# Loads ahead of the masks, row sums of squares on VectorE, a shared transfer rate and an earlier place for the output projections in a planned trunk kernel

## The chip, the cores and the metric

The kernel runs on one core of a Trainium2 chip. The metric is the device time of one execution in microseconds (us). The engines are named as in the profile: PE is TensorE (PEld its weight loads), DVE VectorE, ACT ScalarE, POOL GpSimd, and SP the engine that issues all DMAs here.

## The reference

Two layers of a hybrid trunk over 1024 positions of width 1024, in float32. Every layer normalises, projects into two mixers, projects back, adds the residual, and runs a gated MLP (width 2816) whose gate passes a causal convolution:

```python
for l in range(DEPTH):                       # DEPTH = 2
    h = rms_norm(x, norm_mix_pre[l])
    if l % 2 == 0:
        z = h @ ev_w_in[e]
        ya, v_a = rwkv7_mix(...)             # 8 heads x 64, a recurrence over time
        yb = sgu_mix(...)                    # spatial gating on blocks of 128
        mix = jnp.concatenate([ya, yb], axis=-1) @ ev_w_out[e]
    else:
        z = h @ od_w_in[o]
        yc = hgrn2_mix(...)                  # gated linear recurrence
        yd = gdn_mix(...)                    # gated delta rule
        mix = jnp.concatenate([yc, yd], axis=-1) @ od_w_out[o]
    x = x + rms_norm(mix, norm_mix_post[l])
    h = rms_norm(x, norm_ffn_pre[l])
    x = x + rms_norm(conv_glu_ffn(h, ...), norm_ffn_post[l])
```

## The kernel before

**Tiling.** The positions are cut into two halves of 512 (`TH`); activations lie with the features on the 128 partitions, so a tile is 128x512. A product of float32 accuracy is made of three products of a shorter type: `split` writes the high part of a tile (`h`, or `wh` of a weight; on ScalarE) and the rest (`l`, or `wl`; on VectorE), and `dense` multiplies h by wh, l by wh, and h by wl into a PSUM bank `d`. A block of 128 output columns takes 24 such multiplications over a depth of 1024. All other multiplications (transposes, the recurrences' small products, norms) go into banks `m`.

**Threads and a planner.** `Trunk.run` makes one Python generator ("thread") for each piece of work: `start` (input and first norm), `rows` (transposes of the raw input for the residual), `sgu`, `mixers` (input projections of the recurrent mixers, which put a `unit` for each head pair and quarter of the positions in a queue), `mix` (output projection, post-norm, residual and next norm: `mixed` and `residual`), and `ffn`, each for a layer and a half. `Plan` keeps a model of the engines. At each step it takes of the threads that can run earliest the one with the smallest urgency (`self.urg`; units 0, `mix` 1, `mixers` 2, `ffn` 3) and `place` gives each instruction a start in the model's time, with a cost by engine and shape. The instructions of each engine are then ordered by these starts, and the order is fixed by dependences, so every engine works strictly in the planned order, whatever happens on the chip. A DMA's arrival in the model is its issue plus 1.1 us plus its bytes over a rate.

**A unit.** A recurrent unit inverts triangular 64x64 matrices. The 16x16 blocks of the diagonal are inverted on GpSimd by `inverse_base`, which sends the matrix through DRAM (`ib`, then `iN`), runs 15 steps of two instructions (`itm`, `iPT`), and sends the result back through DRAM (`ir`, `iR`). TensorE and VectorE finish it (`iU`, `iQ`, `iP`), and then a chain of state steps follows over four chunks of 64 positions (`Z`, `WT`, `ST`, `QT`).

**The head.** `setup` makes constants; the masks `lm` of the inversion are made by GpSimd and VectorE from scratch tiles (`low`, `bk16` to `bk64`) of a pool that is closed again, so that its room goes to the pool `tp` opened next, from which all working tiles come. `start(0)` loads x in eight tiles `xt` of 128x512, then a row of column constants (`columns(0)`: `colr`, transposed into `col`), then small parameters, and normalises (`junk`, `ss`, `xr`), transposes (`m<-ident,xr`) and splits the result into `h` and `l`.

**The residual.** `square_sum` squares a tile on ScalarE and adds it to the running sum on GpSimd. In `residual` this is done for the eight 128x512 tiles `row` of a half after each `row` is scaled and added to `xt`; the sum is then reduced over the partitions by TensorE (`m<-ones,sq`), and the next norm's `xn`, `h` and `l` follow. The feed-forward's convolution keeps the last two columns of the gate `g` in `fhalo`: two small GpSimd instructions in each block.

In the profile nearly all instructions have the line L66, that of the recording helper, so they are told apart by their tiles.

Of the kernel before, what the change touches and what calls it, by code (L numbers as in the profile page):

```python
# [9 lines left out]
F32 = mybir.dt.float32  # L10
F32R = mybir.dt.float32r
AF = mybir.ActivationFunctionType
ALU = mybir.AluOpType
# [80 lines left out]
    return key[1] if key[0] == "base" else key  # L94


class Plan:


# [2 lines left out]
    def __init__(self, nc, past=None, tc=None):  # L102
        self.nc, self.past, self.tc = nc, past, tc
        names = ("tensor", "vector", "scalar", "gpsimd", "sync")
        for n in names:
            setattr(self, n, Engine(self, n, getattr(nc, n)))
        self.busy = {n: [(0.0, 0.0)] for n in names}
        self.ready, self.used, self.uses, self.owner = {}, {}, {}, {}
        self.port = {"vector": [], "gpsimd": []}
        self.now, self.cur = 0.0, None  # L110
        self.fresh, self.given = {}, {}
        self.shared, self.ended, self.turns, self.work = {}, set(), {}, {}
        self.order = {}

        self.lives, self.bufs, self.seq, self.spawned = {}, {}, 0, {}
        self.free = {g: [0.0] * n for g, n in past.bufs.items()} if past else None
# [131 lines left out]
    def place(self, eng, method, outs, ins, scaled=False, func=None):  # L248
        c = self.cost(eng, method, outs[0], ins, scaled)
        t = 0.0  # L250
# [8 lines left out]
        for x in outs:  # L259
            if x.space == DRAM:  # L260
                continue
            n = x.tensor.name
# [36 lines left out]
        t = at  # L299
# [21 lines left out]
        if eng == "tensor":  # L321
            self.now = max(self.now, t) if t - c <= self.now + 0.5 else self.now + c
        elif eng == "sync":
            eng = "dma"
            c = max(0.1, outs[0].size() * 4 / (359e3 if min(outs[0].shape[-1], ins[0].shape[-1]) > 64 else 180e3))
            t = begin + 1.1 + c
        for x in outs:
            n = x.tensor.name
            if t >= self.ready.get(n, (0.0, eng))[0]:
# [7 lines left out]
    def start(self, x, threads):  # L337


        t = max(x.wake, self.now)  # L340
        if not self.past:
            return t
        p = x.piece + 1
        need = self.past.need.get((x.key, p), {})
        for g, n in need.items():
            f = self.free[g]
            if len(f) < n:
                return None
            t = max(t, f[n - 1])
        tags = [g for g in need if g in "BCS"]  # L350
        if tags and not self.safe(x, threads):
            return None
        return t
# [66 lines left out]
class Trunk:  # L420
# [30 lines left out]
    def setup(self):  # L451
# [46 lines left out]

        self.lm = [cst.tile([P, 64], F32, name=f"lm{j}") for j in range(2)]
        self.ibufs, self.icount = {}, {}  # L500
        with ExitStack() as c:
            tmp = self.pool("msk", 1, ctx=c)
            low = tmp.tile([64, 64], F32, name="low")
            nc.gpsimd.memset(low, 1.0)
            nc.gpsimd.affine_select(out=low, in_=low, compare_op=ALU.is_gt, fill=0.0, base=0,
                                    pattern=[[-1, 64]], channel_multiplier=1)
            blks = []
            for w in (16, 32, 64):
                b = tmp.tile([64, 64], F32, name=f"bk{w}")
                nc.gpsimd.memset(b, 1.0)  # L510
                v = b.rearrange("p (n w) -> p n w", w=w)
                nc.gpsimd.affine_select(out=v, in_=v, compare_op=ALU.is_ge, fill=0.0, base=0,
                                        pattern=[[-w, 64 // w], [0, w]], channel_multiplier=1)
                nc.gpsimd.affine_select(out=v, in_=v, compare_op=ALU.is_ge, fill=0.0, base=w - 1,
                                        pattern=[[w, 64 // w], [0, w]], channel_multiplier=-1)
                blks.append(b)
            for j in range(2):
                t = self.lm[j]
                nc.vector.tensor_tensor(out=t[0:64], in0=blks[j + 1], in1=blks[j], op=ALU.subtract)
                nc.vector.tensor_tensor(out=t[0:64], in0=t[0:64], in1=low, op=ALU.mult)  # L520
                nc.vector.tensor_tensor(out=t[0:64], in0=self.ident[0:64, 0:64], in1=t[0:64], op=ALU.subtract)
                nc.vector.tensor_copy(t[64:128], t[0:64])


        self.rst = cst.tile([P, NCH, C], F32, name="rst")
# [7 lines left out]
        self.halo = cst.tile([P, 12, 3], F32, name="halo")  # L533
        self.fhalo = cst.tile([P, MFF, 2], F32, name="fhalo")
        self.tp = self.pool("tp")

    def columns(self, part):

# [174 lines left out]
    def square_sum(self, s, x):  # L713

        sq = self.t("sq")
        self.nc.scalar.activation(sq, x, AF.Square)
        if s is None:
            return sq
        self.nc.gpsimd.tensor_tensor(out=s, in0=s, in1=sq, op=ALU.add)
        return s  # L720

    def inv_rms(self, s):
# [1109 lines left out]
        return x  # L1832

    def start(self, hf):
        self.xss[hf] = xs = self.first_loads(hf)
        if hf == 0:
            self.columns(0)
            self.rwkv_lora()
        yield from self.first_norm(hf, xs)
        self.ready.add((0, hf))  # L1840
        if hf == 0:
            self.columns(1)

    def rows(self, hf):
# [3 lines left out]
    def run(self):  # L1848
# [5 lines left out]
            for n in "rgh":  # L1854
                self.st[(n, j, 0)] = None
        self.groups, self.workers, self.ahead = [5, 5, 4, 4, 4], 4, 1
        self.urg = dict(unit=0, mix=1, sgu=1, mixers=2, ffn=3, start=1, rows=2.5)
        threads = []

        def add(kind, l, hf, gen, cond):  # L1860
# [69 lines left out]
```

## Time and profile before

| what | us |
|---|---|
| median of 3 runs (lowest to highest) | 2994.29 (2992.13 to 2996.55) |
| the profiled execution's own time | 2990.66 |
| its span, first to last instruction | 2988.9 |
| mean granted TensorE clock, share of full speed | 0.976 |
| PE busy | 2835.0 (95%) |
| DVE busy | 1810.9 (61%) |
| ACT busy | 1256.0 (42%) |
| POOL busy | 699.8 (23%) |

The span is what the trace covers; the execution's own time is 1.76 us longer. Busy times are sums over the instructions of an engine. A busy PE is not a PE at full speed: where the granted clock is low, the same multiplications take longer and count as busy all the same.

### The profile page before, as it was taken

The numbers are of one execution on the slowest core, as the hardware profiler recorded it, in microseconds if no ns is written. First come the engines' busy times: TensorE is split into PE (matmuls) and PEld (weight loads), VectorE is DVE, ScalarE is ACT, GpSimd is POOL, SyncE is SP. The second block draws the span as 40 slices with busy tenths as digits, with TensorE's granted clock in tenths as the row PEclk, the third lists the DMA queues.
The fourth block names the chain that finished last, engine by engine and source line by source line (L and its number), as shares of the span: only waits on it lengthen the run. The fifth ranks groups of instructions, "written<-read, shape, count | busy, mean of one in ns | idle before, by whom it ended". The sixth has DMA issues, their size and how long they took to land. (4 is left out here: it accounts for less than half of the span.)

```text
span 2988.9 us, 46564 instructions
## 1 busy us (share of the span) xinstructions
PE 2835.0 (95%) x16608; PEld 2281.5 (76%) x16608; DVE 1810.9 (61%) x3654; ACT 1256.0 (42%) x2435; POOL 699.8 (23%) x1624
## 2 busy tenths in 40 slices
PE   6998999889999999999999999999999999999998
PEld 5776777567878878777778878787777788888886
DVE  5747665765565466565665575666676548454444
ACT  4435354444444345433333344543333335444333
POOL 1255242533020020223430121213443112100001
PEclk9999999899999999999999999999999999999999
DMA  5233353322443344535423443363642344343332
GB/s 160 79 85 80 74 145 95 91 53 76 125 131 102 96 128 95 94 58 79 79 67 92 129 134 113 101 107 70 79 83 60 91 122 144 108 125 89 110 95 92
DMA packets 560229, 294.14 MB, mean 98 GB/s; under 512 B 103293, under 2 KB 533198, under 8 KB 559998
## 3 DMA queue, kind: packets, MB, share of 16 engines
q1 hardware_dynamic: 559998, 291.17, 38.6%
q8 instruction: 131, 2.15, 0.3%
q14 instruction: 100, 0.82, 0.1%
HBM read 255.37 MB, written 35.71 MB: 97 GB/s over the span
## 5 line engine op out<-in xcount | busy, mean ns | idle before, releaser
L66 PE MATMUL d<-h,wh 128*128 128x512 f32 (+1 forms) x2544 | 1049.5, 413 | 2.5 <-ACT h L66 2.3
L66 PE MATMUL d<-h,wl 128*128 128x512 f32 (+1 forms) x2544 | 1016.5, 400 | 14.6 <-DVE wl L66 14.5
L66 PE MATMUL d<-l,wh 128*128 128x512 f32 (+1 forms) x2544 | 1014.1, 399 | 0.2 <-DVE l L66 0.2
L66 ACT CAST wh<-wr 128x512 fp32r<-128x512 f32 (+1 forms) x860 | 507.1, 594 | 702.3 <-PE d L66 539.4
L66 DVE TENSOR_TENSOR wl<-wr,wh 128x512 fp32r<-128x512 f32 (+1 forms) x860 | 568.8, 675 | 245.3 <-ACT wh L66 236.5
L66 PEld LDWEIGHTS d<-h,wl 128*128 128x128 f32 (+1 forms) x2544 | 484.3, 190 | 130.5 <-DVE wl L66 17.9
L66 PEld LDWEIGHTS d<-h,wh 128*128 128x128 f32 (+1 forms) x2544 | 485.6, 191 | 110.3 <-ACT h L66 3.7
L66 PEld LDWEIGHTS d<-l,wh 128*128 128x128 f32 (+1 forms) x2544 | 486.0, 191 | 100.3 <-DVE l L66 2.8
L66 PE MATMUL d<-mh,wh 128*128 128x512 f32 x704 | 284.5, 404 | 0.0
L66 PE MATMUL d<-mh,wl 128*128 128x512 f32 x704 | 279.4, 397 | 3.1 <-DVE wl L66 3.1
L66 PE MATMUL d<-ml,wh 128*128 128x512 f32 x704 | 279.4, 397 | 0.0
L66 POOL TENSOR_TENSOR sq<-sq 128x512 f32<-128x512 f32 x97 | 133.9, 1381 | 540.0 <-ACT sq L66 539.7
L66 DVE SCALAR_TENSOR_TENSOR t<-g,col,t 128x512 f32<-128x512 f32 x176 | 137.2, 780 | 184.1 <-ACT t L66 152.4
L66 POOL TENSOR_TENSOR rt<-rt,mhalf 128x4 f32<-128x4 f32 (+1 forms) x94 | 105.8, 1127 | 459.5 <-DVE rt L66 435.7
L66 POOL TENSOR_TENSOR itm<-iN,iPT 16x39 f32<-16x39 f32 (+15 forms) x480 | 164.3, 342 | 192.7 <-DMA iN<-ib 123.0
L66 DVE TENSOR_TENSOR acc<-acc,d 128x512 f32<-128x512 f32 x128 | 88.0, 687 | 144.4 <-PE d L66 143.9
L66 POOL TENSOR_TENSOR iPT<-iPT,itm 16x55 f32<-16x55 f32 (+15 forms) x480 | 166.1, 346 | 36.1
L66 PEld LDWEIGHTS d<-mh,wl 128*128 128x128 f32 x704 | 133.4, 190 | 36.1 <-DVE wl L66 4.8
L66 PEld LDWEIGHTS d<-mh,wh 128*128 128x128 f32 x704 | 133.5, 190 | 30.8 <-issue 0.4
L66 PEld LDWEIGHTS d<-ml,wh 128*128 128x128 f32 x704 | 133.6, 190 | 29.3 <-DVE ml L66 0.3
L66 ACT COPY g<-d 128x512 f32<-128x512 f32 x88 | 51.6, 586 | 154.8 <-PE d L66 154.6
L66 POOL COPY fhalo<-g 128x2 f32<-128x2 f32 x44 | 9.6, 218 | 391.5 <-ACT g L66 369.7
(339 smaller groups left out, 3206.4 us busy)
## 6 DMA issues: line engine op xcount, KB each, us to landing
wr<-in_ffn_w_in SPq DMA_DIRECT2D x352, 256.0 KB
wr<-in_od_w_in SPq DMA_DIRECT2D x128, 256.0 KB
wr<-in_ffn_w_out SPq DMA_DIRECT2D x96, 256.0 KB
wr<-in_ev_w_in SPq DMA_DIRECT2D x84, 256.0 KB
xt<-xd SPq DMA_DIRECT2D x56, 256.0 KB
wr<-in_ffn_w_out SPq DMA_DIRECT2D x64, 192.0 KB
wr<-in_ev_w_out SPq DMA_DIRECT2D x32, 256.0 KB
yl<-yd SPq DMA_DIRECT2D x32, 256.0 KB
```

Of the source, the lines that this page charges most:

```text
L66: r = fn(*args, **kw)
```

## The change

Four edits. `masks` becomes a method of its own whose scratch tiles are ordinary tiles of `tp` (class "S", up to 128 columns), and is called in `start(0)` after the first norm; `columns(0)` is called ahead of the x loads. The running sum of squares is added on VectorE. In the plan, transfers no longer run side by side at 359 (or 180) KB per us each: `fit_in` puts each into the first free gap of one common list, at 300 (or 150) KB per us. And the thread `mix` gets the urgency -1, so that it stands ahead of the units.

```diff
+def fit_in(iv, t, c):
+
+    i = len(iv)
+    while i > 0 and iv[i - 1][1] > t:
+        i -= 1
+    while i < len(iv) and iv[i][0] < t + c:
+        t = max(t, iv[i][1])
+        i += 1
+    iv.insert(i, (t, t + c))
+    if len(iv) > 200:
+        del iv[:100]
+    return t
...
         elif eng == "sync":
             eng = "dma"
-            c = max(0.1, outs[0].size() * 4 / (359e3 if min(outs[0].shape[-1], ins[0].shape[-1]) > 64 else 180e3))
-            t = begin + 1.1 + c
+
+            c = max(0.1, outs[0].size() * 4 / (300e3 if min(outs[0].shape[-1], ins[0].shape[-1]) > 64 else 150e3))
+            t = fit_in(self.moved, begin + 1.1, c) + c
...
-        with ExitStack() as c:
-            tmp = self.pool("msk", 1, ctx=c)
-            low = tmp.tile([64, 64], F32, name="low")
...
+    def masks(self):
+
+        nc = self.nc
+
+        def square(name):
+            return self.t(name, (64, 128))[:, 0:64]
+
+        low = square("low")
...
-        self.nc.gpsimd.tensor_tensor(out=s, in0=s, in1=sq, op=ALU.add)
+        self.nc.vector.tensor_tensor(out=s, in0=s, in1=sq, op=ALU.add)
...
     def start(self, hf):
+        if hf == 0:
+            self.columns(0)
         self.xss[hf] = xs = self.first_loads(hf)
         if hf == 0:
-            self.columns(0)
             self.rwkv_lora()
         yield from self.first_norm(hf, xs)
         self.ready.add((0, hf))
         if hf == 0:
+            self.masks()
             self.columns(1)
...
-        self.urg = dict(unit=0, mix=1, sgu=1, mixers=2, ffn=3, start=1, rows=2.5)
+        self.urg = dict(unit=0, mix=-1, sgu=1, mixers=2, ffn=3, start=1, rows=2.5)
```

Since the planner sets every engine's order, the edits show in the orders of the instructions more than in their number.

The first place is the head of the program, SP's queue. Before, it began so:

```order
L66 DMA xt<-in_x 128x512 x8
L66 DMA wup<-in_rwkv_w_up 32x512
L66 DMA colr<-in_norm_mix_pre 8x128
L66 DMA mu_168<-in_rwkv_mu 64x1
L66 DMA wup<-in_rwkv_a_up 32x512
L66 DMA gup<-in_rwkv_g_up 96x512
L66 DMA mu_168<-in_rwkv_mu 96x1
L66 DMA wr<-in_ev_w_in 128x4x128 x2
```

The column load `colr` stood behind the eight x loads and one small load. The new queue of SP at the same place:

```order
L66 DMA xt<-in_x 128x512 x5
L66 DMA colr<-in_norm_mix_pre 8x128
L66 DMA xt<-in_x 128x512 x3
L66 DMA mu_141<-in_rwkv_mu 64x1
L66 DMA wup<-in_rwkv_w_up 32x512
L66 DMA gup<-in_rwkv_g_up 96x512
L66 DMA wr<-in_ev_w_in 128x4x128 x2
```

The column load moved up between the fifth and the sixth x load, and two small loads moved behind the first two weights `wr`.

The second place is VectorE in the first output projection (layer 0, first half), where each block ends with a copy `row<-d`; `iU`, `ST` and `Z` are steps of units, `wl` weight parts. Before, its second part read:

```order
L66 TENSOR_TENSOR wl<-wr,wh 128x512
L66 COPY row<-d 128x512
L66 TENSOR_TENSOR iU<-m,lm_105 128x256
L66 TENSOR_TENSOR iU<-m,lm_106 128x256
L66 TENSOR_TENSOR wl<-wr,wh 128x512
L66 TENSOR_TENSOR iU<-m,lm_106 128x256
L66 TENSOR_TENSOR wl<-wr,wh 128x512
L66 TENSOR_TENSOR ST<-U_5621,m 64x128
L66 COPY row<-d 128x512
L66 SCALAR_TENSOR_TENSOR Z_5637<-m,dg,Zd 64x64 x2
L66 TENSOR_TENSOR wl<-wr,wh 128x512
```

Between two `row` copies stood up to four steps of units. The new order of VectorE there:

```order
L66 COPY row<-d 128x512
L66 TENSOR_TENSOR wl<-wr,wh 128x512
L66 TENSOR_TENSOR sq<-sq 128x512
L66 TENSOR_TENSOR wl<-wr,wh 128x512
L66 COPY row<-d 128x512
L66 TENSOR_TENSOR wl<-wr,wh 128x512
L66 TENSOR_TENSOR sq<-sq 128x512
L66 TENSOR_TENSOR wl<-wr,wh 128x512
L66 COPY row<-d 128x512
```

No step of a unit stands between the copies any more, and the sums of squares `sq<-sq` are new on this engine.

The third place is GpSimd at the first halo copy of the feed-forward (layer 0, first half). Before, it stood inside an inversion:

```order
L66 TENSOR_TENSOR itm<-iN,iPT 32x8x8
L66 TENSOR_TENSOR iPT<-iPT,itm 32x8x8
L66 TENSOR_TENSOR itm<-iN,iPT 32x7x9
L66 MEMSET g 128x2
L66 COPY fhalo<-g 128x2
L66 TENSOR_TENSOR iPT<-iPT,itm 32x7x9
```

The rows `itm` and `iPT` are steps of one unit's inversion. The new order of GpSimd there:

```order
L66 MEMSET iPT 32x256
L66 MEMSET iPT 32x16
L66 TENSOR_TENSOR rt<-rt,mhalf 128x4 x2
L66 MEMSET g 128x2
L66 COPY fhalo<-g 128x2
L66 TENSOR_TENSOR itm<-iN,iPT 32x15
L66 TENSOR_TENSOR iPT<-iPT,itm 32x15
L66 TENSOR_TENSOR itm<-iN,iPT 32x14x2
```

The first halo copy now stands ahead of the first step of the inversion that follows; the next one (not shown) stands behind nearly all of that inversion's steps.

## Rows read from the trace of the kernel before

**Rows 1.** The page, part 1: busy time, share, instructions of each engine.

```profile
PE 2835.0 (95%) x16608; PEld 2281.5 (76%) x16608; DVE 1810.9 (61%) x3654; ACT 1256.0 (42%) x2435; POOL 699.8 (23%) x1624
```

**Rows 2.** Stretches: length, engines' busy us (instructions), granted clock, DMA share, GB/s.

```profile
0.00:29.66 29.66, 6.81 (x34) 5.67 (x34) 14.78 (x52) 11.61 (x25) 7.62 (x31) 1.00 0.60 171
29.66:100.00 70.34, 70.34 (x348) 56.04 (x346) 40.35 (x95) 32.70 (x62) 4.40 (x4) 1.00 0.41 113
100.00:546.00 446.00, 414.12 (x3510) 330.20 (x3508) 301.88 (x799) 204.03 (x463) 182.41 (x434) 0.96 0.37 99
546.00:622.00 76.00, 51.13 (x439) 37.76 (x438) 42.18 (x95) 24.37 (x53) 45.87 (x126) 0.80 0.24 58
622.00:2988.90 2366.90, 2292.61 (x12287) 1851.87 (x12286) 1411.69 (x2617) 983.35 (x1835) 459.52 (x1031) 0.98 0.40 98
```

**Rows 3.** Waits of SP's queue up to 30 us: total, times, longest.

```profile
SPq L66 <- DVE lm L66: 5.2, 1, 5.2
```

**Rows 4.** Timeline of the head: start, us, engine, operation, idle before and releaser.

```profile
0.88 0.07 DVE L66 MEMSET mhalf<- 128x8 f32 x1 [0.88 <-PEq L1919]
...
6.02 3.72 SPq L66 DMA_DIRECT2D xt<-in_x  x8
...
6.82 0.59 DVE L66 MEMSET colr<- 128x128 f32 x4
8.78 1.28 ACT L66 ACT_TABLE_LOAD   x1 [8.78 <-DMA xt<-in_x]
...
16.62 0.45 PE L66 MATMUL m<-ident,colr 128*128 128x128 f32 x1 [16.62 <-DMA colr<-in_norm_mix_pre]
...
17.10 0.29 DVE L66 COPY col<-m 128x128 f32<-128x128 f32 x1 [5.51 <-PE m L66]
```

**Rows 5.** The page, part 5: busy us, mean ns, idle us before, releaser.

```profile
L66 POOL TENSOR_TENSOR sq<-sq 128x512 f32<-128x512 f32 x97 | 133.9, 1381 | 540.0 <-ACT sq L66 539.7
...
L66 DVE TENSOR_TENSOR acc<-acc,d 128x512 f32<-128x512 f32 x128 | 88.0, 687 | 144.4 <-PE d L66 143.9
```

**Rows 6.** Timelines of four engines from 545 to 555 us.

```profile
545.45 0.63 ACT L66 ACTIVATE sq<-row 128x512 f32<-128x512 f32 x1
...
551.23 1.25 POOL L66 TENSOR_TENSOR sq<-sq 128x512 f32<-128x512 f32 x1
...
552.53 1.87 PE L66 MATMUL m<-ones,sq 128*128 128x1 f32 x8 [6.30 <-POOL sq L66]
...
554.44 0.16 DVE L66 TENSOR_SCALAR rt<-m 128x4 f32<-128x4 f32 x1 [4.85 <-PE m L66]
```

**Rows 7.** Timelines of DVE and POOL in a later residual stage.

```profile
856.95 0.69 DVE L66 TENSOR_TENSOR row<-row,xt 128x512 f32<-128x512 f32 x1
...
859.98 1.31 POOL L66 TENSOR_TENSOR sq<-sq 128x512 f32<-128x512 f32 x1 [7.20 <-ACT sq L66]
...
860.01 1.82 DVE L66 TENSOR_TENSOR row<-row,xt 128x512 f32<-128x512 f32 x1
```

**Rows 8.** Sum of five residual stages (853:882, 1098:1125, 1728:1756, 1868:1896, 2475:2500).

```profile
sum 137.00, PE 122.87 PEld 96.62 DVE 119.17 ACT 70.69 POOL 57.59; mean PE 24.57 PEld 19.32 DVE 23.83 ACT 14.14 POOL 11.52
```

**Rows 9.** The chain that ended last: start, us, what.

```profile
2632.53 322.70 PE d L66 x1392
```

**Rows 10.** Timelines of POOL, DVE and PE from 592 to 614 us.

```profile
592.49 0.70 POOL L66 TENSOR_TENSOR itm<-iN,iPT 32x15 f32<-32x15 f32 x1 [19.65 <-DMA iN<-ib]
...
610.94 1.71 DVE L66 SCALAR_TENSOR_TENSOR t<-g,col,t 128x512 f32<-128x512 f32 x2 [13.38 <-POOL g L66]
...
613.12 0.77 PE L66 MATMUL m<-ST,QT 128*128 128x128 f32 x2 [11.31 <-DVE ST L66]
```

**Rows 11.** Three stretches of small multiplications alone, columns as in rows 2.

```profile
578.60:594.10 15.50, 14.16 (x313) 12.01 (x311) 13.18 (x37) 7.72 (x20) 1.37 (x4) 1.00 0.24 57
241.80:266.50 24.70, 17.26 (x116) 13.91 (x115) 21.09 (x68) 13.40 (x37) 14.81 (x41) 0.72 0.31 92
...
sum 60.30, PE 50.32 PEld 41.38 DVE 45.25 ACT 29.11 POOL 17.84; mean PE 16.77 PEld 13.79 DVE 15.08 ACT 9.70 POOL 5.95
```

More of the change, by code (lines that the diff above doesn't have):

```diff
@@ L109, in __init__ @@
         self.port = {"vector": [], "gpsimd": []}
+        self.moved = []
         self.now, self.cur = 0.0, None
@@ L500, in setup @@
         self.ibufs, self.icount = {}, {}
-        with ExitStack() as c:
-            tmp = self.pool("msk", 1, ctx=c)
-            low = tmp.tile([64, 64], F32, name="low")
[L504 to L522, printed above, removed]
         self.rst = cst.tile([P, NCH, C], F32, name="rst")
@@ L535, in setup @@
         self.tp = self.pool("tp")
+    def masks(self):
[3 more added lines that the diff above has]
+        low = square("low")
+        nc.gpsimd.memset(low, 1.0)
+        nc.gpsimd.affine_select(out=low, in_=low, compare_op=ALU.is_gt, fill=0.0, base=0,
+                                pattern=[[-1, 64]], channel_multiplier=1)
+        blks = []
+        for w in (16, 32, 64):
+            b = square(f"bk{w}")
+            nc.gpsimd.memset(b, 1.0)
+            v = b.rearrange("p (n w) -> p n w", w=w)
+            nc.gpsimd.affine_select(out=v, in_=v, compare_op=ALU.is_ge, fill=0.0, base=0,
+                                    pattern=[[-w, 64 // w], [0, w]], channel_multiplier=1)
+            nc.gpsimd.affine_select(out=v, in_=v, compare_op=ALU.is_ge, fill=0.0, base=w - 1,
+                                    pattern=[[w, 64 // w], [0, w]], channel_multiplier=-1)
+            blks.append(b)
+        for j in range(2):
+            t = self.lm[j]
+            nc.vector.tensor_tensor(out=t[0:64], in0=blks[j + 1], in1=blks[j], op=ALU.subtract)
+            nc.vector.tensor_tensor(out=t[0:64], in0=t[0:64], in1=low, op=ALU.mult)
+            nc.vector.tensor_tensor(out=t[0:64], in0=self.ident[0:64, 0:64], in1=t[0:64], op=ALU.subtract)
+            nc.vector.tensor_copy(t[64:128], t[0:64])
     def columns(self, part):
```

## The prediction

> **What bounds the kernel now.** I read the page's head first. TensorE (PE) is busy for 95% of the span, the next engine, VectorE (DVE), for 61%, GpSimd (POOL) for 23% [rows 1]. So the time is TensorE's work plus its gaps plus the stretches in which its clock is low, and an edit counts only by what it does to these. The table by stretches shows where these lie [rows 2]: 22.9 us of gaps before the first dense multiplication at 29.66; none from there to 100; 31.9 us from 100 to 546, at a mean granted clock of 0.96; 24.9 us in the 76 us from 546 to 622, at 0.80; 74.3 us in the 2366.9 us after that. A clock of 0.80 over 51.13 busy us means that about a fifth of them, 10 us, was lost to the lower of the two levels (1.2 instead of 2.4 GHz). The stretch at 546 thus costs 35 us, the dearest of the kernel for its length.
>
> **Where the change moves things.** In the orders of the two programs TensorE has 13,569 instructions each. From the 4,200th on (about 850 us in the trace of before) fewer than 800 of the remaining 9,300 stand elsewhere; before that nearly every stage is laid out anew. So terms are to be sought in the head, in the first 850 us, and in the sums of squares.
>
> **The head.** SP waited 5.2 us for `lm`, the masks' last results, since the loads' buffers lie where the masks' scratch was [rows 3], and issued the first x load at 6.02 [rows 4]. Now the masks use buffers of their own and the five first loads wait for nothing; VectorE's first instruction, at 0.88, shows when the engines are free to start. That is 5.1 us. The column load `colr` stood behind all eight loads; the transpose that needs it ran at 16.62, the copy `col` behind that at 17.10, and VectorE's normalisation is queued behind this copy. Now `colr` is sixth. It waits for VectorE to clear its buffer, which was done at 6.82 behind the masks and now stands ahead of them; the three loads behind it in SP's queue wait along, but five loads in flight cover that. Before, 2.2 MB landed between 8.78 (the first load's arrival, where ScalarE (ACT) starts) and 16.62, 0.28 MB per us; the first five and `colr`, 1.3 MB, need 4.7 us from about 3.7 on, so `col` comes at 9 to 9.5. From `col` to the first dense multiplication it is 12.56 us (17.10 to 29.66), a chain of VectorE, POOL, TensorE and ScalarE that isn't changed: about 22 instead of 29.66. I take **-7.5 us**, with -5.1 (the wait alone) and -8.3 as bounds. Nothing hides it: TensorE is fully busy for the 70 us behind [rows 2].
>
> **The sums of squares.** 97 additions of 1381 ns leave POOL; on VectorE the same kind, `acc<-acc,d`, takes 687 ns [rows 5], so 67 us are added to an engine with 1178 us free (2988.9 less 1810.9). Two things hang on it. First, POOL does its work in order, and the additions stood among the steps of the triangular inversions. At 545.45 ScalarE starts the last square of a row (0.63 us), POOL adds it only at 551.23 to 552.48, TensorE waits 6.30 us for it, and VectorE lay idle in just that time, 4.85 us before 554.44 [rows 6]. On VectorE the sum would be ready by about 547.3. Secondly the additions slow VectorE even now: while POOL adds at 859.98, VectorE's `row<-row,xt` takes 1.82 us instead of 0.69 [rows 7]. In that residual stage (853 to 882) six of VectorE's operations are stretched, together by some 4.8 us, and seven additions of 0.69 bring 4.8: even. The five such stages from there on hold 14.1 us of gaps (137 us less 122.87), and VectorE is busy for 119.17 of the 137 [rows 8]. I take **0**, with -7 (half of the gaps) and +13 (half of the 27.6 us that 40 additions of 0.69 take, where only 17.8 us are free) as bounds.
>
> The Trainium skill bears on this in two places, which pull against each other. Perfetto Trace Analysis, section Optimizing Scalar/DVE Operations, would offload a saturated VectorE to other engines, GpSimd included, which speaks against this edit; by that rule the residual stages would lose up to the 13 us. SBUF — State Buffer, section Who interferes with whom, says that a VectorE instruction with two SBUF inputs and a GpSimd instruction that reads SBUF exclude each other for their whole length; by that rule POOL's additions were never free for VectorE, and the stages stay even. The trace agrees with the second (1.82 against 0.69).
>
> **The output projections.** `mix` goes from urgency 1 to -1, ahead of the mixers' units (0). Before, 8 blocks of the first projection were mixed with three units' inversions and state steps; now they stand together, 180 of its 192 dense multiplications without a unit's between. Dense multiplications follow each other at 0.232 us (1392 in 322.70 [rows 9]), so units are held by some 42 us and TensorE is full meanwhile: no cost there. The bill comes later: the units' small multiplications run bare. Counted in the new order, between the second row sum of squares and the feed-forward's first blocks stand 260 small multiplications in three runs (183, 20, 57) with 34 dense ones between; before, the longest run there had 163.
>
> **The stretch at 546.** Its 35 us are the 6.30 just named, 11.3 us in one wait at 613, smaller gaps, and 10 us of low clock behind them. The 11.3 us are a chain [rows 10]: GpSimd waited 19.65 us for the load `iN`, so the inversion ran late; the feed-forward's first halo copy, two small POOL instructions, stood behind it; VectorE waited 13.38 us for POOL's `g`, in order, and the state step `ST` behind that held TensorE. In the new order three inversions end ahead of the first halo copy, so that wait goes; but the second halo copy again stands behind nearly a whole inversion. What comes in place: before, three bare runs of 163, 75 and 167 small multiplications took 60.3 us, 0.149 each, the quickest 15.5 us for 163, 0.095 each [rows 11]. 260 at the mean cost 0.054 x 260 = 14 us over that pace; and I leave one POOL wait of 11 us in. So -35 + 14 + 11 = **-10 us**. Bounds: -31 (only 4 us come back) and +26 (all 260 at the pace of the slowest, 24.7 us for 75, 0.33 each, so 61 us).
>
> **The shared transfer rate** adds no instruction; it lets the planner expect loads later when they overlap, so work that waits for them is set later in every queue. That is right in kind for `iN`, but a 32 KB load at the new rate is only some 0.2 us of the plan, against waits of 20 us. I put nothing for it. The rest of 100 to 546, newly ordered, holds 31.9 us of gaps and about 16 us of low clock: **0**, +-10.
>
> **Sum.** -7.5 - 10 + 0 + 0 = -17.5 us. The profiled execution took 2990.66 us with a span of 2988.90; 2973.2 us by it. The median of the runs shown, 2994.29, lies 3.6 us above it; so I predict **2977 us**.
>
> **Rivals.**
> - *All of it comes in* (0.15): the runs go at 0.095 each (-31) and the residual stages gain 7: 2994.3 - 7.5 - 31 - 7 = 2949. For it: TensorE was busy for 14.16 of 15.5 us in the quick run [rows 11].
> - *Slower: the bare recurrences* (0.13): the three held units come due together, with too little dense work to lay between; at 0.33 each +26, with the head +18.5: about 3013. It decides from 0.26 us per small multiplication on, where 35 + 7.5 us are used up (42.5 / 260 + 0.095). For it: the run at 241.8, whose clock was 0.72; against it: that run waited for a VectorE busy for 21 of 24.7 us.
> - *VectorE fills up* (0.12): `wl`, VectorE's part of every weight, comes late for TensorE where VectorE is full, as it is in the five residual stages [rows 8]; +13 gives 2990.
> - *The change does little* (0.15): weights come too late for the earlier start (the same 0.28 MB per us now has to feed TensorE 7.5 us earlier), or new waits take the old ones' place in the new order: -2, 2992.
>
> **How the numbers follow.** The forecast has 0.45, by itself 2966 to 2987. A measurement of this kernel can tell about 0.2%, 6 us, from no change. Faster by more: the forecast, the first rival and a third of the third, 0.65. Slower: the second and a little of the last, 0.15. Same: 0.20. The range, 2946 to 3002, holds all but the second rival.
>
> **What would show it.** Right: SP's first issue near 1 us, `col` near 9.5, first dense multiplication near 22; no POOL wait ahead of `ones,sq`; `row<-row,xt` near 0.69 throughout; no VectorE wait of over 5 us for `g`. Wrong: a stretch between 480 and 640 with a clock under 0.8 and gaps of over 40 us; residual stages with over 20 us of gaps; gaps between 22 and 100 us.

## The result and the profile of the changed kernel

The changed kernel takes **2950.47 us** (median of 4 runs, 2944.84 to 2953.02) against 2995.42 for before in the same comparison: ratio 0.9847, 95% interval 0.9829 to 0.9866. The direction was as forecast and the time lies inside the range, but the move is -45 us where -18 was forecast. The profiled execution has a span of 2951.3 us, 37.6 less than the one of before; the sums below are made against these 37.6.

The page's first part, as [rows 1]:

```profile
PE 2836.7 (96%) x16608; PEld 2285.5 (77%) x16608; DVE 1843.5 (62%) x3747; ACT 1258.8 (43%) x2435; POOL 574.9 (19%) x1527
```

TensorE's busy time is that of before (2835.0); what went are its gaps. VectorE has 32.6 us more, GpSimd 124.9 less.

Five stretches of the changed kernel, columns as in [rows 2]. They are cut at the first dense multiplication, at 100 us, and at the first dense multiplication from the 2,400th and from the 3,000th instruction of TensorE on; before, these two stand at 477.31 and 621.67.

```profile
0.00:22.61 22.61, 7.50 (x34) 6.37 (x34) 14.26 (x52) 11.93 (x25) 7.50 (x31) 1.00 0.84 236
22.61:100.00 77.39, 73.32 (x351) 59.68 (x349) 39.16 (x90) 35.76 (x68) 5.64 (x4) 0.96 0.46 130
100.00:487.68 387.68, 365.78 (x3036) 290.79 (x3034) 270.75 (x724) 178.28 (x399) 142.47 (x372) 0.96 0.36 93
487.68:599.08 111.40, 95.25 (x942) 76.13 (x939) 79.16 (x187) 48.54 (x112) 50.23 (x119) 0.89 0.30 83
599.08:2951.30 2352.22, 2294.89 (x12258) 1852.50 (x12257) 1440.13 (x2697) 984.27 (x1835) 369.09 (x1002) 0.98 0.41 99
```

The head begins 7.1 us earlier, but the stretch behind it, full at a clock of 1.00 before, now has 4.1 us of gaps and a clock of 0.96. The stretch around 546 is still the one with the lowest clock (0.89).

To see where the time went, each dense multiplication of the trace was laid beside its place in TensorE's order, so that two kernels can be compared at the same instruction. The changed kernel is ahead by 7.1 us at the first dense multiplication, by 22.1 at the 4,200th instruction (852.7 before, 830.6 now), by 40.2 at the 9,000th and by 37 from there to the end. So 22 us come from the first 850 us, where the order is new, and some 15 from behind, where the prediction had put nothing. Behind 850 two things stand out. Three residual stages (from 1095, 1725 and 1868 in before's time) go from 116.9 to 104.0 us in sum, and a wait for `K` is gone: from 1555 on, the stretch to the same place in TensorE's order takes 11.8 instead of 21.6 us (13.9 if it is cut at the same dense multiplications). Together that is 22.7, of which some 4.5 are lost again in between and 3 behind the 9,000th.

The head, as [rows 4]:

```profile
0.81 2.29 SPq L66 DMA_DIRECT2D xt<-in_x  x5
...
3.94 0.31 DVE L66 MEMSET colr<- 128x128 f32 x2
...
8.09 0.44 PE L66 MATMUL m<-ident,colr 128*128 128x128 f32 x1 [8.09 <-DMA colr<-in_norm_mix_pre]
...
8.57 0.29 DVE L66 COPY col<-m 128x128 f32<-128x128 f32 x1 [2.66 <-PE m L66]
```

SP issues at 0.81, `col` stands at 8.57, and the first dense multiplication starts at 22.61: the head as it was forecast. The groups of the moved operation and of the row addition (by lines), as [rows 5] and [rows 7]:

```profile
L66 DVE TENSOR_TENSOR sq<-sq 128x512 f32<-128x512 f32 x97 | 67.2, 693 | 23.7 <-ACT sq L66 17.7
L66 DVE TENSOR_TENSOR row<-row,xt 128x512 f32<-128x512 f32 x32 | 22.1, 690 | 0.7
```

67.2 us of additions came to VectorE, but its busy time grew by 32.6 only: its own instructions got shorter. `row<-row,xt` took 979 ns in the mean before and takes 690.

### The profile page after: what moved, and what is told of

Its sections match the earlier page's. It is cut to its first block, busy times and chain, and to the rows that moved or that the text cites. A ratio compares the mean times of both kernels' runs of the same rounds, so it can differ in the third digit from the quotient of the medians.

```text
span 2951.3 us, 46440 instructions
## 1 busy us (share of the span) xinstructions
PE 2836.7 (96%) x16608; PEld 2285.5 (77%) x16608; DVE 1843.5 (62%) x3747; ACT 1258.8 (43%) x2435; POOL 574.9 (19%) x1527
## 5 line engine op out<-in xcount | busy, mean ns | idle before, releaser
L66 DVE TENSOR_TENSOR wl<-wr,wh 128x512 fp32r<-128x512 f32 (+1 forms) x860 | 560.4, 664 | 229.7 <-ACT wh L66 223.2
L66 POOL TENSOR_TENSOR itm<-iN,iPT 32x48 f32<-32x48 f32 (+15 forms) x480 | 160.6, 335 | 172.2 <-DMA iN<-ib 77.5
L66 POOL TENSOR_TENSOR iPT<-iPT,itm 32x48 f32<-32x48 f32 (+15 forms) x480 | 177.9, 371 | 36.2
L66 DVE TENSOR_TENSOR sq<-sq 128x512 f32<-128x512 f32 x97 | 67.2, 693 | 23.7 <-ACT sq L66 17.7
```

The source lines that it names most:

```text
L66: r = fn(*args, **kw)
```

## The experiments

Theory A: the additions on GpSimd held VectorE and came late, and taking them away shortened the residual stages. Theory B: these stages shrank because the new order, by the rate and the urgency, feeds TensorE better there. Later theory C came in: whatever edit makes the planner draw a new order draws a new time with it (such an order with its time is called a draw below); D is its opposite, that an edit's time is its own.

**One edit at a time, on before.** Each edit is that of the diff above:

```diff
# only_sq
-        self.nc.gpsimd.tensor_tensor(out=s, in0=s, in1=sq, op=ALU.add)
+        self.nc.vector.tensor_tensor(out=s, in0=s, in1=sq, op=ALU.add)
# only_mix
-        self.urg = dict(unit=0, mix=1, sgu=1, mixers=2, ffn=3, start=1, rows=2.5)
+        self.urg = dict(unit=0, mix=-1, sgu=1, mixers=2, ffn=3, start=1, rows=2.5)
# only_rate
-            c = max(0.1, outs[0].size() * 4 / (359e3 if min(outs[0].shape[-1], ins[0].shape[-1]) > 64 else 180e3))
-            t = begin + 1.1 + c
+            c = max(0.1, outs[0].size() * 4 / (300e3 if min(outs[0].shape[-1], ins[0].shape[-1]) > 64 else 150e3))
+            t = fit_in(self.moved, begin + 1.1, c) + c
# only_head
-            tmp = self.pool("msk", 1, ctx=c)
+    def masks(self):
...
+            self.columns(0)
         self.xss[hf] = xs = self.first_loads(hf)
```

only_sq: 

> Before with one edit alone: the running sums of squares are added on VectorE. Theory A (the additions on GpSimd held VectorE and came late, so taking them away is what shortened the residual stages behind 850 us, 14.9 us in all over five stages, and the wait for K at 1565): the five residual stages lose 12 to 15 us in sum, row<-row,xt falls from a mean of 0.98 to 0.69 us, the 6.3 us wait ahead of ones,sq goes, and the program takes 2972 to 2982, about 18 us less than before. Theory B (the stages shrank because the new order of the weights' parts, by the rate and the urgency, feeds TensorE there): row<-row,xt falls all the same, but the five stages stay within 4 us of before and the program within 6 us of it.

only_mix: 

> Before with one edit alone: the output projections' thread gets the urgency -1. Theory A: the five residual stages behind 850 us keep their length within 3 us in sum; the first projection stands together, and the stretch around 546 us gets shorter by about 10 us (35 of gaps and low clock, less some 25 that come back while the held units run bare), so about 2985. Theory B: the residual stages shrink by at least half of the 14.9 us here. If the projections' place is worth nothing, the time is that of before within 6 us.

only_rate: 

> Before with one edit alone: transfers in the plan share one list at 300 KB per us. By the prediction's term it is worth nothing: within 6 us of before, with a new order and other waits in the first 850 us. Theory B: the wait for K at 1565 (21.6 us from there to 1575) and the residual stages shrink here, so that 10 to 25 us go behind 850 us. Theory A: those stretches stay as they are.

only_head: 

> Before with one edit alone: the masks' scratch comes from the working tiles, and the column load stands ahead of the x loads. The first dense multiplication comes at 22.6 us instead of 29.7, as in the changed kernel. If the gain lasts, the program takes 7 us less (2987); if the weights' loads can't follow the earlier start, 3 us of it are left by 100 us and the time is that of before within 6 us. Nothing behind 850 us changes by either theory.

Measured, beside 2992.71 for before: only_sq 2969.17 (ratio 0.9927, 0.9914 to 0.9940), only_mix 2980.65 (0.9959, 0.9946 to 0.9972), only_rate 2964.35 (0.9908, 0.9896 to 0.9921), only_head 3012.99 (1.0073, 1.0057 to 1.0090). The three stages behind 850 speak for A: 103.3 us in sum with the additions on VectorE, 114.7 with only_mix, 108.9 with only_rate and 112.2 with only_head, against 116.9. Not all of it fits: A had these stages unchanged with the rate alone, and by both theories the head was to change nothing behind 850, but they lost 8.0 and 4.7 us; and only_sq came out 3 us faster than A's range. The rest was a surprise: the rate, put at nothing, alone gave -28 us, and the head alone cost 20, although its first dense multiplication came 9.1 us earlier.

**The same edits taken out of the changed kernel** (the hunks above, reversed).

no_sq: 

> The changed kernel with the sums of squares back on GpSimd. Theory A (the additions on GpSimd held the residual stages): the stages that began at 1095, 1725 and 1868 in the trace of before get back to within 2 us of their old lengths (44.95, 39.95, 32.00; 116.9 in sum against 104.0 in the changed kernel), and the program takes 15 to 25 us more than the changed one: 2966 to 2976. Theory B (the new order of the weights did it): these stages stay at 104 within 4 us in sum, and the program within 8 us of the changed one.

no_mix: 

> The changed kernel with the output projections' urgency back at 1. If each edit has a worth of its own, that of its run alone (12 us): about 2962, and the difference lies between 480 and 640 us, where the projection is again mixed with units. If the first 850 us are a matter of which order the planner happens to fall into (theory C), the difference may have either sign and up to 20 us, and lies anywhere in the first 850 us; the rest stays as in the changed kernel.

no_rate: 

> The changed kernel with the old transfer rates of the plan. If the rate has a worth of its own, that of its run alone (28 us): about 2979, of which 11 us in the first 850 us and the rest behind. By the prediction's term (nothing): 2950 within 8 us. Theory C: either sign, up to 20 us, in the first 850 us.

no_head: 

> The changed kernel with the old head. The first dense multiplication is back at 29.7 us. If each edit has a worth of its own, that of its run alone (the head cost 20 us): about 2930, faster than the changed kernel by 20 us. If the head is worth the 7 us by which the first dense multiplication comes earlier, and the 27 us that its run alone lost later are those of the order it fell into (theory C): 2958 within 10 us.

Measured, beside 2992.77: no_sq 2963.36 (0.9898, 0.9883 to 0.9914), no_mix 2977.73 (0.9948, 0.9935 to 0.9961), no_rate 2981.29 (0.9959, 0.9946 to 0.9972), no_head 2949.79 (0.9858, 0.9842 to 0.9874). The stages are at 111.7 in no_sq and between 103.5 and 105.5 in the others: A again in kind but not in size, since it had 116.9 within 2 and no_sq itself at 2966 or more. B falls as the main cause of these stages. no_rate came out where its run alone had it, no_mix neither there nor within theory C's 20 us, and no_head within theory C's range (2958 within 10) and not at the 2930 of separate worths. The worths don't add up. An edit is worth one thing alone and another beside the others: the squares 23.5 and 13 us, the projections' place 12 and 27, the head -20 and about 0. Only the rate had the same worth twice, 28 and 31. That needed a control.

**An edit that should be worth nothing.** In the planner's model a transfer lands at its issue plus 1.1 us plus its bytes over the rate. The 1.1 was changed by 0.02 or 0.04:

```diff
# b_lat, on before (b_lat2: 1.08, b_lat3: 1.14)
-            t = begin + 1.1 + c
+            t = begin + 1.12 + c
# a_lat, on the changed kernel (a_lat2: 1.08, a_lat3: 1.14)
-            t = fit_in(self.moved, begin + 1.1, c) + c
+            t = fit_in(self.moved, begin + 1.12, c) + c
# unshared_300, on before
-            c = max(0.1, outs[0].size() * 4 / (359e3 if min(outs[0].shape[-1], ins[0].shape[-1]) > 64 else 180e3))
+            c = max(0.1, outs[0].size() * 4 / (300e3 if min(outs[0].shape[-1], ins[0].shape[-1]) > 64 else 150e3))
```

b_lat: 

> Before, with the planner's fixed part of a transfer at 1.12 instead of 1.1 us and nothing else: an edit that should be worth nothing by itself, but gives the planner other numbers and so another order. Theory C (any new order of the first 850 us draws a new time there, and so the single edits' times of -28 to +20 us hold much chance): the time differs from before by 8 to 20 us, either sign, nearly all of it in the first 850 us. Theory D (an edit's time is its own, and order by order there is little between): within 6 us of 2992.7.

a_lat: 

> The changed kernel with the same small edit, 1.12 instead of 1.1 us. Theory C: 8 to 20 us away from 2950.5, either sign, in the first 850 us; the stages at 1095, 1725 and 1868 stay at 104 us in sum. Theory D: within 6 us.

a_lat2: 

> The changed kernel with 1.08 instead of 1.1 us. As for 1.12: 8 to 20 us away by theory C, within 6 us by theory D. If the changed kernel is a lucky draw, both come out slower, by some 10 us in the mean.

unshared_300: 

> Before with transfers at 300 (150) KB per us, but side by side as before, so that only the number of the rate edit is made, not the sharing. If the sharing is what is worth 28 us, the time is that of before within 6 us. If the slower number is enough, about 2965. By theory C: anywhere within 20 us of before, and then the rate's 28 us aren't to be put down to the sharing.

Measured, beside 2990.76: b_lat 2964.15 (0.9916, 0.9903 to 0.9930), a_lat 2979.32 (0.9962, 0.9949 to 0.9975), a_lat2 2964.18 (0.9917, 0.9903 to 0.9930), unshared_300 2977.39 (0.9956, 0.9943 to 0.9970). unshared_300 lies between its two expectations. But the edit that means nothing moved before by -27 us and the changed kernel by +29 and +14: theory C. In size and place C was off: it had 8 to 20 us, nearly all in the first 850 us, but by the profiled spans only 7.2 of b_lat's 20.8 us lie there, and 12.3 of a_lat's 28.8. D falls, and with it every reading of a single edit's time that doesn't look behind it, the rate's 28 us included.

**The order held, the engine changed.** A third kind of handle was given to the additions, which the planner places and costs as the one engine's while they run on the other. TensorE's, ScalarE's and SP's orders stay as they were, row for row:

```diff
-    def __init__(self, plan, name, eng):
+    def __init__(self, plan, name, eng, like=None):
...
+        self.adder = Engine(self, "vector", nc.vector, "gpsimd")   # fixed_before_v
+        self.adder = Engine(self, "gpsimd", nc.gpsimd, "vector")   # fixed_after_g
...
-            t = self.plan.place(self.name, method, outs, aps + ins,
+            t = self.plan.place(self.like, method, outs, aps + ins,
...
+        self.nc.adder.tensor_tensor(out=s, in0=s, in1=sq, op=ALU.add)
```

fixed_before_v: 

> Before in its own order, unchanged on TensorE, ScalarE and SP: only the 97 additions of squares are planned as GpSimd's and run on VectorE at the same places. So the execution of this edit is seen without a new order. Theory A (the additions on GpSimd held VectorE and came late in the residual stages): the stages from 1095, 1725 and 1868 go from 116.9 to about 104 us in sum, the 6.3 us wait ahead of ones,sq goes, and the program takes 10 to 20 us less than before: 2972 to 2982. If the single edit's 23 us were those of its new order (theory C alone): the stages stay within 3 us, the program within 6 us of before.

fixed_after_g: 

> The changed kernel in its own order, with the 97 additions planned as VectorE's and run on GpSimd at the same places, at 1381 instead of about 690 ns each. Theory A: the three stages go from 104 to 112 us or more, and the program takes 10 to 20 us more than the changed one: 2960 to 2970. Theory C alone: within 6 us of 2950.5.

Measured: fixed_before_v 2987.40 (0.9986, 0.9977 to 0.9995, beside 2990.72), fixed_after_g 2958.44 (0.9891, 0.9877 to 0.9905). In before's order the engine alone is worth 3 to 4 us, less than the 10 to 20 of theory A; in the changed kernel's order 8 us by the medians, 13 by the two ratios, 3 by the profiled spans. The three stages in the four kernels, columns as in [rows 2]: first before, then fixed_before_v, then the changed kernel, then fixed_after_g.

```profile
1095.02:1139.97 44.95, 42.28 (x177) 33.93 (x176) 38.12 (x50) 21.92 (x38) 12.48 (x11) 0.92 0.47 147
1725.06:1765.01 39.95, 34.94 (x150) 27.84 (x149) 30.94 (x40) 19.48 (x33) 13.02 (x11) 0.96 0.47 145
1868.10:1900.10 32.00, 29.28 (x126) 23.31 (x125) 26.50 (x33) 15.61 (x29) 12.90 (x13) 0.95 0.48 148
```

```profile
1093.44:1134.58 41.14, 39.66 (x177) 31.73 (x176) 35.20 (x56) 22.19 (x38) 2.02 (x3) 1.00 0.49 158
1723.71:1762.63 38.92, 34.98 (x150) 27.78 (x149) 29.65 (x46) 19.46 (x33) 1.15 (x2) 0.96 0.48 148
1865.80:1895.14 29.34, 27.87 (x125) 22.16 (x124) 24.71 (x41) 15.80 (x27) 1.82 (x5) 1.00 0.52 161
```

```profile
sum 104.00, PE 100.91 PEld 80.59 DVE 90.36 ACT 55.36 POOL 6.47; mean PE 33.64 PEld 26.86 DVE 30.12 ACT 18.45 POOL 2.16
```

```profile
sum 108.68, PE 101.61 PEld 80.35 DVE 94.34 ACT 55.28 POOL 34.48; mean PE 33.87 PEld 26.78 DVE 31.45 ACT 18.43 POOL 11.49
```

With the order held, the three stages lose 7.5 us (116.90 to 109.40, where theory A had 104) in the one direction and gain 4.7 in the other. VectorE is busy for less with the additions than without them (35.20 against 38.12, with six more instructions), and in the first and third stage TensorE's clock is 1.00 instead of 0.92 and 0.95, where its gaps got shorter. The wait ahead of `ones,sq` goes with the engine, too: 6.30 us for GpSimd before, 1.30 us and no longer for GpSimd in fixed_before_v, none in the changed kernel, and 10.56 us for GpSimd in fixed_after_g. First fixed_before_v, then fixed_after_g:

```profile
551.35 1.02 PE L66 MATMUL m<-ones,sq 128*128 128x1 f32 x8 [1.30 <-DVE z L66]
```

```profile
524.28 1.86 PE L66 MATMUL m<-ones,sq 128*128 128x1 f32 x8 [10.56 <-POOL sq L66]
```

So A's mechanism is shown, and its price for the program is small: in fixed_before_v, 4.4 of the 7.5 us were lost again between 1325 and 1500 us, where the same instructions ran at 0.96 instead of 1.00 in part, at longer gaps. The mean of one row addition follows the engine in each order. First before, then fixed_before_v, then fixed_after_g; the changed kernel's 690 stands above:

```profile
L66 DVE TENSOR_TENSOR row<-row,xt 128x512 f32<-128x512 f32 x32 | 31.3, 979 | 1.0
```

```profile
L66 DVE TENSOR_TENSOR row<-row,xt 128x512 f32<-128x512 f32 x32 | 22.3, 697 | 0.8
```

```profile
L66 DVE TENSOR_TENSOR row<-row,xt 128x512 f32<-128x512 f32 x32 | 28.0, 874 | 0.9
```

The wait for `K` goes with the order and not with the engine. Where before and fixed_before_v wait, the stretch from 1555 takes 21.6 and 21.0 us, in the changed kernel and fixed_after_g 11.8 and 11.8. b_lat2 below, which is before with 0.02 us less in the planner's model, doesn't have this wait either, so it is part of a draw. First before, then fixed_before_v, by TensorE's timeline:

```profile
1565.40 0.66 PE L66 MATMUL m<-ident,K 128*128 128x128 f32 x2 [6.34 <-DVE K L66]
```

```profile
1564.44 0.66 PE L66 MATMUL m<-ident,K 128*128 128x128 f32 x2 [6.36 <-DVE K L66]
```

**More draws of both kernels.**

b_lat2: 

> Before with the planner's fixed part of a transfer at 1.08 instead of 1.1 us. Theory C: another draw, 5 to 30 us away from 2992.7; if before is an unlucky draw, faster than it, 2965 to 2985. If only 1.12 was a lucky exception: 2993 within 6 us.

b_lat3: 

> Before with 1.14 instead of 1.1 us. Theory C: another draw; with before and the draws at 1.08 and 1.12 it gives the spread of this kernel's orders, about 10 us around a mean of 2975 to 2985, beside which the 42 us between the two kernels are to be read. If orders matter little: within 6 us of 2992.7.

a_lat3: 

> The changed kernel with 1.14 instead of 1.1 us in a transfer's planned time. Theory C: one more draw; with 2950, 2979 and 2964 it gives the mean of the changed kernel's orders. If before's four draws (2991, 2964, 2988, 2999; mean 2985) and these have the same mean, this one comes out near 3045, which nobody expects; I expect 2950 to 2980, so a mean difference of about 20 us, half of the 42 us measured between the two kernels.

no_head_lat2: 

> The changed kernel with the old head, and 1.08 instead of 1.1 us. If the head edit keeps its 7 us, draws without it are slower: 2960 to 2985. In the traces so far every kernel with the new head starts its dense multiplications 7 to 9 us earlier and has lost that by about 107 us, to a 4.1 us wait for the second column load and to a lower granted clock; then draws without it have the same mean as draws with it, and this one lies between 2940 and 2975, and may be the fastest of all.

Measured: b_lat2 2987.66 (0.9990, 0.9980 to 1.0000), b_lat3 2998.93 (1.0027, 1.0016 to 1.0037), a_lat3 3002.50 (1.0034, 1.0021 to 1.0048), no_head_lat2 2948.12 (0.9852, 0.9838 to 0.9865). a_lat3 is the miss: the changed kernel with 1.14 for 1.1 is slower than before, where 2950 to 2980 was expected. no_head_lat2 isn't to be told from the changed kernel (0.9847), so no run beats it clearly.

The draws side by side, in us. "To 4,200" is the time at TensorE's 4,200th instruction, "behind" the time from there to the 9,000th, "stages" the three stages.

| planned time of a transfer | before | to 4,200 | behind | stages | changed | to 4,200 | behind | stages |
|---|---|---|---|---|---|---|---|---|
| 1.08 | 2987.7 | 846.3 | 1111.2 | 115.6 | 2964.2 | 843.9 | 1096.2 | 104.0 |
| 1.10 (the kernels compared) | 2992.7 | 852.7 | 1111.3 | 116.9 | 2950.5 | 830.6 | 1093.1 | 104.0 |
| 1.12 | 2964.2 | 845.5 | 1101.4 | 111.6 | 2979.3 | 843.0 | 1096.3 | 103.1 |
| 1.14 | 2998.9 | 863.8 | 1103.8 | 115.1 | 3002.5 | 885.2 | 1089.0 | 102.7 |
| mean | 2985.9 | 852.1 | 1106.9 | 114.8 | 2974.1 | 850.7 | 1093.7 | 103.5 |

The means differ by 12 us, and the four draws of a kernel scatter by 15 and 22 us (standard deviations), so a difference of means is good to about 13 us, and these 12 can't be told from nothing. In the first 850 us the means are equal (852.1 and 850.7): the 22 us by which the changed kernel is ahead there, and the 33 by which a_lat3 is behind before, are draws. What holds over draws lies between the 4,200th and the 9,000th instruction: there the two columns don't overlap, neither in the whole stretch (1101.4 to 1111.3 against 1089.0 to 1096.3) nor in the stages. Of the other orders with the additions on GpSimd, only_rate takes 1092.9 there. And from the 9,000th instruction to the end the changed kernel is the slower one in the mean (1031.5 against 1026.6), so that some 8 of the 13 us are left at the end.

What a draw looks like, in the stretch around the output projection (before, from the 2,400th to the 3,000th instruction; then b_lat and a_lat3, each cut at the first dense multiplication from these two instructions on, so that the work in them differs somewhat), columns as in [rows 2]:

```profile
477.31:621.67 144.36, 118.79 (x865) 91.35 (x863) 98.79 (x240) 61.69 (x137) 71.35 (x165) 0.89 0.32 86
```

```profile
493.18:619.40 126.22, 116.83 (x843) 91.77 (x841) 100.72 (x238) 61.36 (x134) 65.75 (x157) 0.99 0.33 89
```

```profile
493.02:647.30 154.28, 124.82 (x907) 100.50 (x905) 101.58 (x259) 60.00 (x135) 56.21 (x145) 0.82 0.28 79
```

b_lat has 9.4 us of gaps at 0.99 where before has 25.6 at 0.89; a_lat3, with the same four edits as the changed kernel, has 29.5 at 0.82. Gaps and low clock come together in all three.

## Why the prediction was right or wrong

**The step that failed** is the size of two terms that it put at zero. "I take 0" for the five residual stages is off by 14.9 us in the pair (12.9 in the three named), beyond its bound of -7; and for the first 850 us, "newly ordered", it took the planned order's own worth as +-10, where the four draws of the changed kernel scatter from 831 to 885 us at the 4,200th instruction (814 to 885 over the 20 kernels profiled). What the runs showed in their place: with the order held, the engine alone takes 7.5 us off the three stages, and an edit of 0.02 us in the planner's model moves the time by 3 to 29 us. The wait for `K` had no term at all. Of the 27 us by which the move was larger than forecast, the residual stages and the `K` wait (13 and 10, of which 7 or so were lost again) make up 15 behind 850, the better draw ahead of it some 5, and the medians' distance, wider by 7 than that of the profiled spans, the rest.

*The head, -7.5.* Right at the first dense multiplication (-7.1) and nearly gone soon after. Behind the 288th dense multiplication the two kernels are level, at 111.00 and 110.80 us. First before, then the changed kernel:

```profile
29.66:111.00 81.34, 81.34 (x427) 64.94 (x424) 49.99 (x124) 37.81 (x73) 6.90 (x5) 1.00 0.44 127
```

```profile
22.61:110.80 88.19, 84.07 (x425) 67.98 (x422) 49.13 (x126) 38.67 (x73) 5.64 (x4) 0.96 0.40 115
```

"Nothing hides it" was the wrong sentence: it took the order behind the head as given. Much the same work takes 6.9 us more: 4.1 in one wait, and 2.7 at a lower clock around it. By TensorE's timeline:

```profile
43.65 0.87 PE L66 MATMUL m<-ident,colr 128*128 128x128 f32 x3 [4.07 <-DMA wr<-in_ev_w_in]
44.32 5.72 PE L66 MATMUL m<-ident,xt 128*128 128x128 f32 x28
```

Transposes of the later column loads and of `xt` now stand at 43.65, behind the 72nd dense multiplication, while SP issues the last two of these loads only at 40.94 and 41.38, behind weight loads. The releaser named is a weight; nine of the eleven orders with such a wait name a column load. Before, the column transposes stood behind the 97th dense multiplication, at 52.25, without a wait, and those of `xt` behind 100 us. It isn't the earlier start that makes the wait: three orders with the old head (only_rate, no_head and no_head_lat2) have it too, 3.9 to 4.3 us long, also behind the 72nd. First only_rate, then no_head:

```profile
50.25 0.87 PE L66 MATMUL m<-ident,colr 128*128 128x128 f32 x3 [4.26 <-DMA colr<-in_hgrn_norm_g]
```

```profile
49.13 0.88 PE L66 MATMUL m<-ident,colr 128*128 128x128 f32 x3 [3.88 <-DMA colr<-in_hgrn_norm_g]
```

The head edit alone (only_head) and the rate edit alone (only_rate) each bring this place of the transposes. Eight kernels with the new head, all with the wait, have done 288 dense multiplications at 109.8 us in the mean, the three with the old head and the wait at 115.7, the seven with the old head and without it at 110.7 (the two held orders left out). So beside orders with the same wait the new head keeps 5.9 of the 6.3 us by which it starts earlier, and the new place of the transposes costs about as much. That is the rival "the change does little", come true in this term alone, by new waits in the new order and not by loads too late for the earlier start. Behind this the lead comes and goes with each order's waits: in the pair it is 8.9 us four dense multiplications later, and behind the 400th, kernels with the new and the old head stand at 163.8 and 163.4 us in the mean.

*The sums of squares, 0.* The forecast weighed one stage, that at 853, found it even, and took that for all five. With before's order held that stage is even indeed (46.60 and 46.50 us); so is the last (34.35 and 34.04). The three between are not (-3.8, -1.0, -2.7). Over all orders, nine kernels with the additions on VectorE have these three at 103.7 us in the mean (102.7 to 105.5), nine with them on GpSimd at 113.0 (108.9 to 116.9): -9.3, with no overlap. The first and the third do not overlap by themselves either (40.3 to 40.4 us against 43.4 to 45.0, and 28.5 to 28.6 against 31.4 to 32.1); the second does (33.8 to 36.7 against 33.8 to 40.2), so its 4.8 us in the pair are for the most part a draw. Half to four fifths of the 9.3 is the engine (4.7 and 7.5 with the order held); that the rest comes from a plan that knows where the additions run is argued and not shown. The 6.30 us wait ahead of `ones,sq` went as foreseen, and by the engine.

The rule of the Trainium skill that spoke for "even" (SBUF — State Buffer, section Who interferes with whom: a VectorE instruction with two SBUF inputs and a GpSimd instruction on SBUF exclude each other) agrees with the held orders: 979 against 697 ns for `row<-row,xt`, with nothing changed but the additions' engine. The "even" that the prediction drew from it doesn't: the three stages got 7.5 us shorter. The offloading rule of the Trainium skill (Perfetto Trace Analysis, section Optimizing Scalar/DVE Operations), by which the prediction had the stages lose up to 13 us, was read in part only: the section goes on to say that GpSimd shares an SBUF read port with VectorE, so that offloading between these two might not help. With this the trace agrees: VectorE's busy time in the three stages fell from 95.57 to 89.57 us with the additions on it.

*The output projections and the stretch at 546, -10.* They do stand together, and units' multiplications do run bare behind them. From the 2,000th to the 4,200th instruction the pair differs by 14.6 us (449.0 and 434.3). Over orders, nine kernels with the urgency at -1 take 440.1 us there in the mean and nine with 1 take 449.4, with a scatter of 15 and 12: 9.4 us apart and so near the forecast, but a difference of such means is good to some 6.5 us, so it is neither shown nor refuted. VectorE's 13.38 us wait for `g` and the 11.31 us wait for `ST` [rows 10] aren't there in the changed kernel. Slower bare recurrences, the rival on the other side, came near in a draw: a_lat3, with this stretch at 0.82, ended at 3002.5 where that rival had 3013; that the bare runs alone did it was not shown.

*The other rivals.* "All of it comes in" gave 2949, nearly the time measured, but by 31 us at 546 and 7 in the stages, where the pair has 22 in the whole of the first 850 us and 15 in the stages: the time agrees, the way doesn't. "VectorE fills up" falls with the busy times above.

*The shared rate, 0.* Its two runs gave 28 and 31 us, in contrasts of single draws; one of 0.02 us in another number gave 27 and 29. So 0 can't be refuted, and the runs don't show that the sharing itself is worth anything: this stays open.

*What the prediction did not have* is that before is one draw, and not a good one (2964 by a change of 0.02 us), while the changed kernel is its best of four. The forecast of the mean, -18, is nearer to the -12 of the draws than to the -45 of the pair; but that was luck of its terms, too: its head (-7.5) hardly lasts, and the residual stages, where it put nothing, are the one part that holds over draws.

## What to carry to other kernels

Where a planner turns numbers into an order, change a number that should mean nothing before crediting an edit: here 0.02 to 0.04 us of a model's latency moved the time by up to 52 us, more than the four edits did. To price an edit of the machine's work, hold the order and change only the engine; to price an edit of the plan, compare means of several draws. And read each of several like stages in the trace: the one that was read closely was the one where the edit was worth nothing.

## What the runs showed of the hardware that was not expected

Moving 66.9 us of additions to VectorE, in an order otherwise held, raised its busy time by 30.8 only (1810.9 to 1841.7): 36 us of its busy time before went with GpSimd's additions. And a lower granted clock often stands beside longer gaps: in the stage at 1095, where the sequence of TensorE's instructions was the same, 2.7 us of gaps stand beside a mean clock of 0.92 and 1.5 us beside 1.00. The sum of the gaps alone doesn't settle it, since in the second stage of fixed_after_g 3.5 us of gaps stand beside 1.00; which causes which was not tried.

```profile
1695.04:1732.01 36.97, 33.49 (x150) 26.64 (x148) 31.80 (x42) 17.79 (x32) 9.50 (x9) 1.00 0.46 143
```
